# Attention on negated logits with one scaling a group, products issued in twos beside it, and the second tile's plain products in the sample's PSUM bank

## The chip, the cores and the metric

One core of one Trainium2 chip runs the whole step in one launch. The metric is the device time of that launch in microseconds. The kernel before took 1602.3 us, the median of three runs (1600.12, 1602.30, 1605.38).

## What is computed

One layer of a decoder trunk for 1024 prompt tokens and 8 x 4 sample tokens, d_model 1024, all in float32. The input projection has 9472 columns. Branch A is a gated linear recurrence (HGRN2, 8 heads). Branch B, which the change is about, is sliding-window attention with 16 query heads, 2 key-value heads of 64 channels, window 128, a learned sink for each head and a relative bias:

```python
def sink_softmax(logits, mask, sink):
    logits = jnp.where(mask, logits, -jnp.inf)
    m = jnp.maximum(jnp.max(logits, axis=-1, keepdims=True), sink)
    p = jnp.exp(logits - m)
    return p / (jnp.sum(p, axis=-1, keepdims=True) + jnp.exp(sink - m))
...
    logits = jnp.einsum('bnqkgd,bnskd->bnkgqs', qb, kk) * (B_HD ** -0.5)
    logits = logits + rel_bias_heads(rel, rel_bias)
    probs = sink_softmax(logits, mask, sink.astype(f32).reshape(B_KV_HEADS, B_GROUP, 1, 1))
    out = jnp.einsum('bnkgqs,bnskd->bnqkgd', probs, vv)
```

Both branches are gated and projected, merged, projected again, normalised and added to the residual. The projections behind the input projection (line 1391 on) are not touched.

## The kernel before

**Pairs.** The input projection goes by pairs of 128 output columns (`pair_gemm`, line 374). A pair is computed for two tiles of 512 tokens by Strassen-like products P1 to P7 over six of the eight blocks of the inner dimension; the two others go through `plain`. Every float32 operand is split into a high and a low part, so a product is three passes, and P1 to P7 are nine matmuls of 128 x 512 each, a `plain` six. All of them are recorded at line 380. In the rows, `HT`, `HB`, `LT`, `LB` with `wh`, `wl` are products of P1 to P7, `HR`, `LR` with `wrh`, `wrl` are `plain` ones.

**Banks.** Three PSUM banks `g0` to `g2` take the products, and a fourth, `gs`, has one buffer. `sample_products` (line 358) writes the 32 sample tokens' partial sums into it, ACT copies them out (line 365), and `sample_outputs` (line 368) writes the sums back into the same bank (line 370), from where the two epilogues of the pair read them. In the recurrence's pairs, `turned` (line 716) also allocates `gs`: it transposes the value projection, 32 sample rows first (line 730), then 128 x 512 tiles (line 734).

**Order within a pair** (lines 439 to 467): P1, the sample's products, P5, P6, `sample_outputs`, the second column block's plain products for the first tile (line 452, six matmuls), which DVE adds to the kept P5 (line 453), P3 with its plain, P7, P2 with its plain, P4 with its plain.

**Other work between the matmuls.** TensorE's order is the program's order. After every `quantum` matmuls of a pair, `tick()` (line 206) advances three queues of generators; a generator that yields n sleeps n ticks. Beside the heads of the recurrence (quantum 6) runs `hgrn_chain` (line 833); beside the eight attention pairs (line 1321) and the last four pairs (`gate_b`, line 1357) the quantum is `A_QUANTUM`, and attention is advanced: strip c has the query heads c and c + 8 and four groups of 256 queries. `rows_` (line 1206) issues `logits(g)` and sleeps `A_WAIT[0]` ticks; `outs` (line 1214) waits until the group's logits are issued, sleeps `A_WAIT[1]`, transposes the first half of the weights (`turn`, part 0), sleeps `A_WAIT[2]`, the second half, sleeps `A_WAIT[3]`, multiplies with the values, and sleeps `A_WAIT[4]`. An epilogue that must not run ahead of attention turns the queues itself (`settle`, line 1316). The other engines' orders are made by a scheduler from the recorded program.

**One group of attention.** TensorE writes two banks `lp` (lines 1151, 1155). DVE adds the relative bias and takes the row maximum against the sink, four times 128 x 256 (line 1159), negates the maxima (1161), adds the sink (1163, twice). ACT takes the exponentials with the negated maximum as bias and sums them (1167), and that of the sink (1164). DVE adds, inverts and scales (1169, 1170, 1172, four times). TensorE transposes through one bank `pt` (1182), ACT copies it out (1186), TensorE multiplies with the values (1197), DVE gates (1203). The query tile `stk` that the next strip's logits read is made by ACT (1334) and DVE (1335) out of the pair's first result (413).

## Time and profile before

| what | value |
|---|---|
| median of three runs | 1602.3 us |
| the profiled execution's own time | 1597.13 us |
| its span, first to last instruction | 1595.3 us |
| TensorE busy | 1519.1 us, 95% of the span |
| VectorE (DVE) busy | 956.5 us, 60% |
| ScalarE (ACT) busy | 667.2 us, 42% |
| GpSimd (POOL) busy | 415.9 us, 26% |
| mean granted TensorE clock | 0.978 of full speed |

The profile is of one execution. "Busy" of TensorE is modelled from pipelined matmuls. PEclk is the clock that was granted to TensorE, as a share of full speed. A group's row names line, engine and operation, then output and inputs by the program's names with shapes, then the count, then busy time and the mean of one in ns, then the engine's idle time just before them and what ended it. A row of the timeline has start and duration in us, and in brackets the idle time before it.

### The profile page before, as it was taken

What the parts mean: (1) busy time and instruction counts of PE and PEld (TensorE: products, weight loads), DVE (VectorE), ACT (ScalarE), POOL (GpSimd) and SP (SyncE); (2) the same over time, 40 slices, a digit from 0 to 9 for tenths busy, and PEclk for the clock granted to TensorE, in tenths of its full rate; (3) what the DMA queues carried; (4) which work ended last, traced back from release to release, by engine and by line L of the source; (5) the groups of instructions that cost most, each with busy time, mean ns of one, the idle gap of its engine ahead of it and who ended that gap; (6) DMA issues with size and microseconds to landing.
All of it is one profiled execution on the core that took longest, in us unless ns stands there. A gap on an engine that the chain in (4) does not pass through costs nothing. (4 is left out here: it accounts for less than half of the span.)

```text
span 1595.3 us, 27896 instructions
## 1 busy us (share of the span) xinstructions
PE 1519.1 (95%) x10569; PEld 1274.6 (80%) x10569; DVE 956.5 (60%) x2221; ACT 667.2 (42%) x1671; POOL 415.9 (26%) x381
## 2 busy tenths in 40 slices
PE   8999999999999999999789999999899999998998
PEld 8777777777787877777567677777699999997998
DVE  8777767575858585854567766764352244227532
ACT  6235343444444435354555555654331122333422
POOL 1374434444343435345111211213000000004100
PEclk9999999999999999999899999999989999998999
DMA  5212121213131212123111111133664544103321
GB/s 181 67 36 87 43 82 53 82 41 95 41 96 30 80 55 82 54 63 79 44 44 47 47 48 47 41 92 91 211 218 142 142 122 145 58 24 101 106 81 55
DMA packets 197250, 129.56 MB, mean 81 GB/s; under 512 B 46323, under 2 KB 184748, under 8 KB 197100
## 3 DMA queue, kind: packets, MB, share of 16 engines
q1 hardware_dynamic: 196300, 127.54, 26.8%
q8 instruction: 83, 1.36, 0.4%
q14 instruction: 51, 0.42, 0.1%
q0 software_dynamic: 672, 0.18, 0.1%
q10 hardware_dynamic: 144, 0.07, 0.0%
HBM read 96.89 MB, written 31.88 MB: 81 GB/s over the span
## 5 line engine op out<-in xcount | busy, mean ns | idle before, releaser
L268 POOL TENSOR_TENSOR wl<-raw,wh 128x384 fp32r<-128x384 f32 x106 | 113.6, 1074 | 272.1 <-ACT wh L267 246.8
L380 PE MATMUL g<-HT,wh 128*128 128x512 f32 x420 | 175.7, 418 | 0.0
L380 PE MATMUL g<-LT,wh 128*128 128x512 f32 x420 | 164.7, 392 | 0.0
L380 PE MATMUL g<-HT,wl 128*128 128x512 f32 x420 | 164.5, 392 | 0.0
L380 PE MATMUL g<-HB,wh 128*128 128x512 f32 x342 | 145.6, 426 | 9.5 <-DVE p L453 9.5
L380 PE MATMUL g<-HB,wl 128*128 128x512 f32 x342 | 136.4, 399 | 0.0
L380 PE MATMUL g<-LB,wh 128*128 128x512 f32 x342 | 136.2, 398 | 0.0
L268 DVE TENSOR_TENSOR wl<-ws,wh 128x384 fp32r<-128x384 f32 x136 | 94.8, 697 | 56.5 <-ACT wh L267 55.4
L267 ACT CAST wh<-ws 128x384 fp32r<-128x384 f32 x136 | 69.6, 512 | 128.1 <-PE g L380 88.1
L380 PE MATMUL g<-HR,wrh 128*128 128x512 f32 x288 | 120.8, 419 | 0.0
L380 PE MATMUL g<-HR,wrl 128*128 128x512 f32 x288 | 113.7, 395 | 0.0
L380 PE MATMUL g<-LR,wrh 128*128 128x512 f32 x288 | 113.1, 393 | 0.0
L380 PEld LDWEIGHTS g<-HT,wh 128*128 128x128 f32 x420 | 79.0, 188 | 33.4 <-issue 7.3
L267 ACT CAST wh<-raw 128x384 fp32r<-128x384 f32 x110 | 56.4, 514 | 106.4 <-PE g L380 97.9
L1571 POOL TENSOR_TENSOR yT<-yT,acc 128x1056 f32<-128x1056 f32 x4 | 12.9, 3262 | 319.4 <-ACT acc L1567 319.4
L380 PEld LDWEIGHTS g<-HT,wl 128*128 128x128 f32 x420 | 79.0, 188 | 17.7
L380 PEld LDWEIGHTS g<-HB,wh 128*128 128x128 f32 x342 | 65.8, 192 | 32.2 <-DVE p L453 12.5
L380 PEld LDWEIGHTS g<-LT,wh 128*128 128x128 f32 x420 | 79.3, 189 | 12.9
L1411 ACT CAST wh<-raw 128x1024 fp32r<-128x1024 f32 (+1 forms) x40 | 36.8, 920 | 124.0 <-PE g L1433 119.8
L380 PEld LDWEIGHTS g<-HB,wl 128*128 128x128 f32 x342 | 65.8, 192 | 15.1
L1412 DVE TENSOR_TENSOR wl<-raw,wh 128x1024 fp32r<-128x1024 f32 (+1 forms) x40 | 46.4, 1162 | 47.8 <-ACT wh L1411 47.8
L380 PEld LDWEIGHTS g<-LB,wh 128*128 128x128 f32 x342 | 66.0, 193 | 10.9
(392 smaller groups left out, 3986.4 us busy)
## 6 DMA issues: line engine op xcount, KB each, us to landing
raw<-in_w_in_dram SPq DMA_DIRECT2D x116, 256.0 KB
raw<-in_w_in_dram SPq DMA_DIRECT2D x64, 128.0 KB
oa_d<-G SPq DMA_DIRECT2D x8, 528.0 KB
oar<-oa_d SPq DMA_DIRECT2D x8, 528.0 KB
sga<-ga_d SPq DMA_DIRECT2D x8, 528.0 KB
obr<-ob_d SPq DMA_DIRECT2D x8, 528.0 KB
ma_d<-sga SPq DMA_DIRECT2D x8, 528.0 KB
gbr<-gb_d SPq DMA_DIRECT2D x8, 528.0 KB
```

What stands on the lines that cost most here:

```text
L267: S.copy(h, x)
L268: eng.tensor_tensor(l, x, h, op=ALU.subtract)
L380: T.matmul(ps, a, b, start=start, stop=stop, skip_group_check=True)
L1411: S.copy(wh[:, :kt, :], raw3)
L1412: V.tensor_tensor(wl[:, :kt, :], raw3, wh[:, :kt, :], op=ALU.subtract)
L1571: G.tensor_tensor(yT[i], yT[i], rb_, op=ALU.mult)
```

## The change

Five edits:

- Query tiles are scaled by -0.125 and the bias table by -1, so that DVE adds negated logits and keeps their minimum against a negated sink `nsink`. The minimum serves as the exponential's bias as it stands, with scale -1; the negation goes, and the two additions of the sink become one.
- The four scalings of a group become one `tensor_tensor` of 128 x 1024 with a broadcast operand (two for the first group of a strip).
- `turn` copies part 0 with DVE, part 1 with ACT as before.
- `A_QUANTUM` goes from 3 to 2 and `A_WAIT` from (5, 2, 2, 1, 2) to (7, 2, 2, 3, 1).
- The second column block's plain products for the first tile are written to bank `gs`; the third bank is no longer used at that place.

```diff
-A_QUANTUM = 3
-A_WAIT = (5, 2, 2, 1, 2)
+A_QUANTUM = 2
+A_WAIT = (7, 2, 2, 3, 1)
...
         if R:
-            b = bank(tb)
+            b = psg.tile([P, HT], F32, name=tname("g"), tag="gs", bufs=1)
             plain(b, 1, 0, True)
             V.tensor_tensor(p5, b, p5, op=ALU.add)
...
-        V.tensor_copy(rel, b[:16, :384])
+        V.tensor_scalar(rel, b[:16, :384], -1.0, None, op0=ALU.mult)
...
+    nsink = sp.tile([P, 16], F32, name="nsink", tag="ssh")
+    V.tensor_scalar(nsink, sink, -1.0, None, op0=ALU.mult)
...
-                    V.tensor_tensor_reduce(lg[:, j, w, lo:], bs[j][:, os], hank[:, j, ::-1][:, lo:], 1.0, sink[:, c + 8 * j:c + 8 * j + 1],
-                                           ALU.add, ALU.max, mx[:, 0, 2 * j + w:2 * j + w + 1])
-            V.tensor_scalar(mx[:, 1, :], mx[:, 0, :], -1.0, None, op0=ALU.mult)
-            for j in range(2):
-                V.tensor_scalar(mx[:, 2, 2 * j:2 * j + 2], mx[:, 1, 2 * j:2 * j + 2], sink[:, c + 8 * j:c + 8 * j + 1], None, op0=ALU.add)
+                    V.tensor_tensor_reduce(lg[:, j, w, lo:], bs[j][:, os], hank[:, j, ::-1][:, lo:], 1.0, nsink[:, c + 8 * j:c + 8 * j + 1],
+                                           ALU.add, ALU.min, mx[:, 0, 2 * j + w:2 * j + w + 1])
+            jw = lambda a: a.rearrange("p (j w) -> p j w", j=2)
+            V.tensor_tensor(jw(mx[:, 2, :]), jw(mx[:, 0, :]), jw(sink)[:, :, c:c + 1].broadcast_to([P, 2, 2]), op=ALU.add)
...
-                S.activation(lg[:, j, w, lo:], lg[:, j, w, lo:], AF.Exp, bias=mx[:, 1, 2 * j + w:2 * j + w + 1],
+                S.activation(lg[:, j, w, lo:], lg[:, j, w, lo:], AF.Exp, bias=mx[:, 0, 2 * j + w:2 * j + w + 1], scale=-1.0,
...
-            for j, w, lo in ji:
-                V.tensor_scalar(lg[:, j, w, lo:], lg[:, j, w, lo:], mx[:, 2, 2 * j + w:2 * j + w + 1], None, op0=ALU.mult)
+            mj = jw(mx[:, 2, :])
+            for ws, lo in ((slice(0, 2), 0),) if g else ((slice(0, 1), 128), (slice(1, 2), 0)):
+                l = lg[:, :, ws, lo:]
+                V.tensor_tensor(l, l, mj[:, :, ws, None].broadcast_to(list(l.shape)), op=ALU.mult)
...
-            S.copy(pT[:, :, lo:], b3[:, :, lo:])
+            (S.copy if part else V.tensor_copy)(pT[:, :, lo:], b3[:, :, lo:])
...
-                S.activation(s[r, j, :], ps[r], AF.Copy, scale=0.125)
-                V.scalar_tensor_tensor(s[o, j, :], ps[r], 0.125, s[r, j, :], op0=ALU.mult, op1=ALU.subtract)
+                S.activation(s[r, j, :], ps[r], AF.Copy, scale=-0.125)
+                V.scalar_tensor_tensor(s[o, j, :], ps[r], -0.125, s[r, j, :], op0=ALU.mult, op1=ALU.subtract)
```

From line 1104 on, lines of the changed kernel stand up to three further down (1182 becomes 1185).

Up to the last key-value pair, no engine's order of instructions changes but by the one negation of the sink; what changes there is who waits. Here is TensorE in the second pair of recurrence head 1, from the middle of the plain products at line 452 on; names in brackets are the engines whose progress a row waits for. Before:

```order
L380 MATMUL g185_1827<-LR7_282,wrh166_1711 128x512
L380 MATMUL g185_1827<-HR6_281,wrl167_1712 128x512
L866 MATMUL d186_1831<-QP1_1536,K1_1535 32x80 [waits DVE_49,PE_49]
L866 MATMUL d186_1831<-QP1_1536,K1_1535 32x80 x31
...
L380 MATMUL g176_1773<-HB228_294,wh171_1747 128x512 [waits Activation_49]
L380 MATMUL g176_1773<-LB229_295,wh171_1747 128x512
L380 MATMUL g176_1773<-HB228_294,wl172_1748 128x512
L730 MATMUL gt190_1892<-cst_118,ts183_1822 32x128 [waits PE_49,Activation_49]
```

And after:

```order
L380 MATMUL g185_1827<-LR7_282,wrh166_1711 128x512
L380 MATMUL g185_1827<-HR6_281,wrl167_1712 128x512 [waits DVE_49]
L866 MATMUL d186_1831<-QP1_1536,K1_1535 32x80 [waits DVE_49]
L866 MATMUL d186_1831<-QP1_1536,K1_1535 32x80 x31
...
L380 MATMUL g176_1773<-HB228_294,wh171_1747 128x512
L380 MATMUL g176_1773<-LB229_295,wh171_1747 128x512
L380 MATMUL g176_1773<-HB228_294,wl172_1748 128x512
L730 MATMUL gt190_1892<-cst_118,ts183_1822 32x128 [waits DVE_49]
```

The transposition of the sample's values (`gt`, line 730, bank `gs`) waited for readers of the sample's sums on ACT; now it waits for DVE, whose addition at line 453 is the last reader of the plain products (`g185`) that hold the bank.

In the third pair of the same head, where the plain products follow the sample's sums. Before, and then after:

```order
L748 MATMUL d224_2174<-cst_118,K1_1535 32x128 [waits Activation_49]
...
L370 MATMUL gs212_2107<-cst_118,part213_2116 128x32 x2
L380 MATMUL g228_2193<-HR6_281,wrh205_2001 128x512
L380 MATMUL g228_2193<-LR7_282,wrh205_2001 128x512
L380 MATMUL g228_2193<-HR6_281,wrl206_2002 128x512
```

```order
L748 MATMUL d224_2174<-cst_118,K1_1535 32x128 [waits Activation_49]
...
L370 MATMUL gs212_2107<-cst_118,part213_2116 128x32 x2
L380 MATMUL g228_2193<-HR6_281,wrh205_2001 128x512 [waits Activation_49]
L380 MATMUL g228_2193<-LR7_282,wrh205_2001 128x512
L380 MATMUL g228_2193<-HR6_281,wrl206_2002 128x512
```

The order is the same, and the first plain product has got a wait for ACT, which reads the sample's sums out of the bank.

TensorE in attention, ahead of the transposition (`pt5_1_0`) of strip 5's second group, whose logits are `lp5_1`. Before, with the rows between left out (the logits of group 3, `lp5_3`, are already issued):

```order
L1155 MATMUL lp5_3_1_10331<-KL_7711,stk5_1_10090 128x256
L380 MATMUL g1259_10206<-HR6_281,wrh1250_10101 128x512
L380 MATMUL g1259_10206<-LR7_282,wrh1250_10101 128x512
...
L1197 MATMUL po5_0_10361<-pTs_7970,vN_7712 64x128 x2
L380 MATMUL g1252_10170<-HT34_268,wh1260_10207 128x512
...
L1182 MATMUL pt5_1_0_10394<-cst_118,lg5_1_10119 128x128 x4
L1182 MATMUL pt5_1_1_10400<-cst_118,lg5_1_10119 128x128 x4
```

After:

```order
L1157 MATMUL lp5_1_1_10043<-KL_7711,stk5_0_9950 128x256
L380 MATMUL g1241_10002<-HR6_281,wrl1217_9711 128x512
L380 MATMUL g1241_10002<-HR6_281,wrh1216_9710 128x512
L380 MATMUL g1241_10002<-LR7_282,wrh1216_9710 128x512
L380 MATMUL g1241_10002<-HR6_281,wrl1217_9711 128x512
L380 MATMUL g1218_9777<-HT490_1234,wh1235_9913 128x512
L380 MATMUL g1218_9777<-LT491_1235,wh1235_9913 128x512
L380 MATMUL g1218_9777<-HT490_1234,wl1236_9914 128x512
L380 MATMUL g1218_9777<-HT490_1234,wh1235_9913 128x512
L380 MATMUL g1218_9777<-LT491_1235,wh1235_9913 128x512
L380 MATMUL g1218_9777<-HT490_1234,wl1236_9914 128x512
L1185 MATMUL pt5_1_0_10097<-cst_118,lg5_1_10040 128x128 x4
```

Before, 66 matmuls of line 380 and the logits of two further groups stand between `lp5_1` and `pt5_1_0`; after, ten matmuls and nothing else. From strip 1 on, the four groups of a strip have 6, 10, 11 and 16 matmuls of line 380 between their logits and their first transposition; the third has in addition a product with the values and the sample's products, the fourth a product with the values and the sample's sums. The first group's logits come four matmuls behind the last plain product of P3.

## The prediction

> **What bounds the kernel now.** The page's first rows, then the windows of two stages, recurrence and attention strips.

> ```profile
> span 1595.3 us, 27896 instructions
> ...
> PE 1519.1 (95%) x10569; PEld 1274.6 (80%) x10569; DVE 956.5 (60%) x2221; ACT 667.2 (42%) x1671; POOL 415.9 (26%) x381
> ...
> 130.00:745.00 615.00, 596.57 (x4761) 471.56 (x4761) 421.59 (x864) 269.04 (x713) 259.00 (x245) 1.00 0.22 65
> 754.00:1050.00 296.00, 271.80 (x1585) 202.25 (x1586) 206.68 (x681) 166.32 (x489) 53.02 (x53) 0.95 0.18 45
> ```

> In a window's row, after its bounds and length stand the busy times of TensorE's matmuls, its weight loads, DVE, ACT and POOL, then the granted clock. TensorE is busy for 97% of the recurrence and 92% of attention, so a wait of TensorE is added time and work elsewhere is hidden while it keeps ahead. The execution took 1597.13 us, 1.8 more than its span and 5.2 less than the median of the runs. What TensorE waits for, in attention (first three rows) and in the whole run (the last):

> ```profile
> PE pt L1182 <- ACT pTs L1186: 11.3, 6, 2.2
> PE pt L1182 <- DVE lg L1172: 7.2, 2, 4.5
> PE lp L1151 <- DVE stk L1335: 4.3, 9, 0.9
> ...
> PE g L380 <- DVE p L453: 9.5, 7, 1.4
> ```

> Total, times and longest follow the colon. Attention also loses clock, 5% of 296 us, 14.8. So all that this change could win by shorter waits is 11.3 + 7.2 + 4.3 + 9.5 + 14.8 = 47 us.

> **The bank.** The plain products of line 452 now wait until both epilogues have read the sample's sums, and whoever takes the bank next waits for line 453. The second pair of a head:

> ```profile
> 409.36:419.92 10.56, 9.24 (x103) 7.13 (x101) 10.54 (x21) 2.56 (x7) 5.97 (x6) 1.00 0.18 51
> ...
> 409.81 0.48 PE L380 MATMUL g<-HR,wrh 128*128 128x512 f32 x1
> ...
> 410.09 0.20 ACT L811 ACTIVATE G<-gs 128x32 f32<-128x32 f32 x1
> ...
> 413.54 0.27 PE L730 MATMUL gt<-cst,ts 128*32 128x128 f32 x1
> ...
> 418.21 0.39 PE L380 MATMUL g<-HT,wl 128*128 128x512 f32 x1
> ...
> 419.15 0.77 DVE L453 TENSOR_TENSOR p<-g,p 128x512 f32<-128x512 f32 x1
> ...
> 419.97 0.51 PE L380 MATMUL g<-HB,wh 128*128 128x512 f32 x1 [1.38 <-DVE p L453]
> ```

> DVE is busy for 10.54 of the 10.56 us up to the end of line 453: it works off the recurrence's chain, which stands ahead in its order, unchanged. Today only P2 waits for that addition, 1.38 us. After, the transposition at 413.54 waits until 419.92, and behind it on TensorE stand P3's last six matmuls, its plain and P7, which run until 418.60 today, 5.06 us. P2 no longer waits, so it starts 5.0 us later; DVE then waits for P3 and stays as far behind TensorE as now. The wait of 0.5 us for the sample's readers (to 410.29) falls inside. Seven heads: 35.0 us.

> The other two pairs of a head wait for the sample's readers alone (third pair, first pair, and the first pair of head 1, where DVE still makes the differences of the input tiles):

> ```profile
> 440.56 0.48 PE L380 MATMUL g<-HR,wrh 128*128 128x512 f32 x1
> ...
> 441.73 0.21 ACT L821 ACTIVATE ct<-gs 128x32 f32<-128x32 f32 x1
> ...
> 470.47 0.48 PE L380 MATMUL g<-HR,wrh 128*128 128x512 f32 x1
> ...
> 471.86 0.17 DVE L773 TENSOR_TENSOR QP<-gs,ct 128x8 f32<-128x8 f32 x1
> ...
> 137.69 0.48 PE L380 MATMUL g<-HR,wrh 128*128 128x512 f32 x1
> ...
> 142.18 0.16 DVE L773 TENSOR_TENSOR QP<-gs,ct 128x8 f32<-128x8 f32 x1
> ```

> 441.94 less 440.56 is 1.4, seven times; 472.03 less 470.47 is 1.6, six times; 142.34 less 137.69 is 4.65 once. That is 9.8 + 9.6 + 4.65 = 24 us. The key-value pair and the last pairs, by the 0.5 us above, make 2. Sum of the bank's waits: 61 us.

> **The clock after a wait.** A wait of 1.99 us, and TensorE's rows some microseconds later:

> ```profile
> 949.73 0.66 PE L1182 MATMUL pt<-cst,lg 128*128 128x128 f32 x4 [1.99 <-ACT pTs L1186]
> ...
> 951.70:955.11 3.41, 3.41 (x18) 2.39 (x17) 2.52 (x13) 0.89 (x3) 0.74 (x1) 0.50 0.04 12
> ...
> 954.23 0.63 PE L380 MATMUL g<-LB,wh 128*128 128x512 f32 x1
> ...
> 954.66 0.60 PE L380 MATMUL g<-HB,wl 128*128 128x512 f32 x1
> ...
> 955.34 0.40 PE L380 MATMUL g<-LB,wh 128*128 128x512 f32 x1
> ...
> 955.57 0.40 PE L380 MATMUL g<-HB,wl 128*128 128x512 f32 x1
> ```

> For 3.41 us the clock is granted at half, and matmuls follow each other by 0.43 us in place of 0.23: 3.41 x (1 - 0.23 / 0.43) = 1.6 us lost. The waits of 1.38 us brought none (the recurrence's window has a clock of 1.00). I charge 1.6 for each new wait of about 2 us or more: seven second pairs and the one of 4.65, so 8 x 1.6 = 13. The bank costs 74 us. [...]

> **Twos and the new waits.** Today a group's softmax has 66 matmuls of cover. Only the first strip shows what it takes uncovered, the first group with 9 matmuls between, the second with 15:

> ```profile
> 762.63 0.47 PE L1182 MATMUL pt<-cst,lg 128*128 128x128 f32 x1 [4.53 <-DVE lg L1172]
> ...
> 769.31 0.50 PE L1155 MATMUL lp<-KL,stk 64*128 64x256 f32 x4
> ...
> 770.04 0.48 DVE L1159 CUSTOM_DVE_ANT_0 lg<-lp,hank,sink 128x256 f32<-128x256 f32 x1
> ...
> 771.26 0.48 DVE L1159 CUSTOM_DVE_ANT_0 lg<-lp,hank,sink 128x256 f32<-128x256 f32 x1
> ...
> 772.71 0.51 ACT L1167 ACTIVATE lg<-lg,mx 128x256 f32<-128x256 f32 x1 [0.24 <-DVE mx L1161]
> ...
> 775.10 0.18 DVE L1170 RECIPROCAL mx<-mx 128x4 f32<-128x4 f32 x1
> ...
> 775.65 1.14 DVE L1172 TENSOR_SCALAR lg<-lg,mx 128x256 f32<-128x256 f32 x4
> ...
> 776.15 1.03 PE L1182 MATMUL pt<-cst,lg 128*128 128x128 f32 x4 [2.69 <-DVE lg L1172]
> ```

> From the logits' end at 769.81 to the last scaling at 776.79 are 7.0 us, and TensorE waited 4.53 and 2.69. After the change every group is like these, with less cover. What the edits take from the chain: without the negation the exponentials start behind the first reduction in place of the fourth. With free engines: reductions to 1.75 us after the logits, exponentials to 2.5, the sink's to 2.7, sum and reciprocal to 3.1, scaling to 4.3. The scaling itself wins nothing; the rows for it and for what else stands in the queues:

> ```profile
> L1412 DVE TENSOR_TENSOR wl<-raw,wh 128x1024 fp32r<-128x1024 f32 x32 | 39.7, 1244 | 44.3 <-ACT wh L1411 44.3
> ...
> L268 DVE TENSOR_TENSOR wl<-ws,wh 128x384 fp32r<-128x384 f32 x136 | 94.8, 697 | 56.5 <-ACT wh L267 55.4
> ...
> L413 DVE TENSOR_TENSOR ct<-g,u 128x512 f32<-128x512 f32 x34 | 23.6, 693 | 31.6 <-PE g L380 31.5
> ...
> L1335 DVE SCALAR_TENSOR_TENSOR stk<-ct,stk 64x512 fp32r<-64x512 f32 x32 | 21.9, 686 | 3.9 <-ACT stk L1334 3.2
> ...
> L1334 ACT ACTIVATE stk<-ct 64x512 fp32r<-64x512 f32 x32 | 20.1, 629 | 16.9 <-DVE ct L413 16.5
> ```

> One scaling of 1.2 us stands for four that took 1.14 together, and TensorE could start behind the first of those. The engines are not free: their orders put other work inside the chain. For a strip:

> - First group: reductions to 1.5, exponentials and a weight cast on ACT to 2.9, the sink's to 3.1; then DVE has a weight split, the sum, a gate (0.69) and the reciprocal to 4.7, the scaling to 5.8. Cover 6 x 0.23 = 1.4; wait 4.4.
> - Second: reductions to 1.8, line 413 to 2.5, on ACT half of the query tile to 3.2 and the sink's to 3.4; on DVE half of the query tile to 4.0, the sum, the other half to 4.8, the reciprocal, the scaling to 6.2. Cover 10 x 0.23 = 2.3; wait 3.9.
> - Third: two weight splits stand ahead of the last three reductions, which end at 2.6; a gate to 3.3, a cast and the sink's on ACT to 4.2, another split to 4.6, sum and reciprocal to 4.9, scaling to 6.1. Cover 11 x 0.23, a product with the values (some 0.8) and the sample's (1.0), 4.2; wait 1.9.
> - Fourth: 4.3, but DVE has the sample's last reader behind the scaling, and the bank keeps TensorE for that: 4.9 against 4.0; wait 0.9.
> - Query tile: the strip's first logits stand four matmuls (0.9) behind the result that they need, by way of lines 413, 1334 twice and 1335: 0.69 + 1.26 + 0.69 and some latency, 3.0; wait 2.1.

> Sum 13.2 a strip. Three of these bring half clock that is not itself covered: 4.8. Eight strips: 8 x 18.0 = 144. What goes is today's 11.3 + 7.2 + 4.3 + 14.8 = 38. Net +106. POOL and the loads are a product further ahead of TensorE and gain time from every wait; the bias tables are issued a strip ahead as now. DVE's part-0 copy, at line 453's 0.7 us, fits the four matmuls before part 1.

> **Sum.** 1597.1 + 74 + 106 = 1777; the medians lie up to 5 us above, so I say 1780. Bounds: the chain at 4.3 everywhere gives waits of 2.9 + 2.0 + 0.1 + 0.9 + 2.1 = 8.0 with two half clocks, 8 x 11.2 - 38 = +52; at today's 7.0, 5.6 + 4.7 + 2.8 + 3.0 + 2.1 = 18.2 with four, 8 x 24.6 - 38 = +159. The bank is 61 without any half clock and 84 if the six waits of 1.6 have it too. So 1597 + 61 + 52 = 1710 to 1597 + 84 + 159 = 1840. Of the rivals I take in the one at 1703, and say 1700 to 1835.

> **Rivals.**

> - Faster: the shorter chain and the even spacing end today's waits, and none take their place: 1597 - 47 = 1550. Decides if the chain falls below its cover of 1.4 to 4.2 us and line 453 comes before the transposition. Against it, four reductions alone take 1.7, and DVE has 10.5 us of work ahead of line 453. Chance 0.02.
> - Attention comes out even, its waits as long as today's: 1597 + 74 = 1671. It needs a chain of about 3 us; no row is that short. 0.06.
> - The bank costs nothing, since the scheduler's work ahead of line 453 is not what holds it: 1597 + 106 = 1703. Against it, DVE's unbroken 10.54 us. 0.05.
> - The half clock stays on through attention: some 34 us of matmuls a strip at half rate lose 34 x 0.47 = 16 in place of 4.8, 8 x 11 = 90 more, 1870. In the rows it ends within 3.4 us once TensorE is dense. 0.07.
> - [...] 0.10. [...]
> - Both parts stay covered and nothing changes: 1602, for the reasons of the first rival less likely still. 0.01.

> My forecast has the other 0.69; outside the range lie 0.02 + 0.06 + 0.07 + 0.01 = 0.16. A measurement tells about 0.3%, 5 us, from no change: faster 0.02, same 0.01, slower 0.97.

> **What would show it.** Right: line 730 waiting for line 453 some 6 us, seven times; `HR` products waiting for lines 821 and 773; `pt` part 0 waiting 4 us for the scaling in the first two groups of every strip; the attention window some 400 us in place of 296, its clock about 0.9. Wrong: the last pairs or the projections behind them longer, the first transpositions of a group without waits, or line 453 early on DVE.

## The result and the profile after

The changed kernel takes 1782.1 us (median of four runs, 1780.5 to 1783.2) against 1602.4 for the kernel before: a ratio of 1.112, 95% interval 1.110 to 1.114. The profiled execution took 1781.36 us. The page's head, and its row of the granted clock in 40 slices:

```profile
span 1779.6 us, 27734 instructions
...
PE 1578.7 (89%) x10569; PEld 1307.9 (73%) x10569; DVE 956.5 (54%) x2102; ACT 656.2 (37%) x1639; POOL 425.8 (24%) x381
...
PEclk9999999999999999998888888889997999999999
```

The attention slices, 19 to 27, stand at 8 where the others stand at 9, but for one, slice 31 right behind the last pairs, where the kernel before dips too. The windows of four stages follow: the recurrence from head 1's first sums of the sample on with the key-value pair, the eight strips, the last pairs, the rest. Columns as in the prediction: bounds, length, busy times of TensorE's matmuls and weight loads, DVE, ACT and POOL, then the clock.

```profile
143.64:823.94 680.30, 612.05 (x4742) 482.48 (x4740) 411.07 (x857) 264.33 (x698) 254.08 (x242) 0.96 0.19 58
823.94:1231.63 407.69, 320.89 (x1685) 229.45 (x1684) 219.90 (x591) 164.25 (x488) 62.92 (x58) 0.86 0.14 36
1231.63:1314.96 83.33, 76.52 (x463) 59.61 (x461) 33.55 (x81) 30.50 (x70) 20.30 (x20) 0.98 0.43 135
1314.96:1779.60 464.64, 443.22 (x2711) 430.31 (x2709) 190.19 (x304) 131.99 (x222) 23.92 (x9) 0.97 0.36 109
```

The same stages of the kernel before:

```profile
137.33:746.44 609.11, 592.41 (x4741) 468.63 (x4740) 415.57 (x856) 264.21 (x698) 255.33 (x244) 1.00 0.22 65
746.44:1051.40 304.96, 279.98 (x1624) 208.71 (x1623) 210.31 (x685) 169.84 (x497) 58.43 (x58) 0.95 0.19 47
1051.40:1132.64 81.24, 81.24 (x524) 63.20 (x523) 37.88 (x107) 37.07 (x94) 19.40 (x20) 1.00 0.37 117
1132.64:1595.30 462.66, 443.00 (x2711) 430.57 (x2709) 189.46 (x304) 131.32 (x222) 23.95 (x9) 0.97 0.38 114
```

So +71.2 in the recurrence, +102.7 in attention, +2.1 in the last pairs, +2.0 in the rest, and +6.3 ahead of 143.64: 184.3 together. What TensorE waits for now (total, times, longest):

```profile
PE pt L1185 <- DVE lg L1175: 65.7, 31, 3.9
PE gt L730 <- DVE p L453: 36.0, 7, 5.2
PE lp L1153 <- DVE stk L1338: 13.8, 16, 1.3
PE g L380 <- DVE QP L773: 12.6, 7, 3.0
PE g L380 <- ACT ct L821: 8.9, 7, 1.3
...
PE ckp L1261 <- DMA cK<-in_cache_swa_k_dram: 5.4, 1, 5.4
...
PE g L380 <- POOL wl L268: 4.9, 1, 4.9
...
PE g L380 <- DVE zS L1354: 4.8, 8, 0.6
PE g L380 <- ACT G L811: 2.8, 7, 0.5
```

The first transposition of the first three groups of every strip waits for the scaling, the transposition of the sample's values waits for line 453, and the readers of the sample's sums hold the plain products up. The wait of P2 for line 453 is gone. Of the rows that the prediction did not have, the 4.9 us for POOL stand at 64.7 in the start-up; of the other traces only no_bank's shows them, and most kernels without them have the same code there, so they are not laid to the change. The second pair of head 4 in the changed kernel, TensorE and DVE:

```profile
449.99 0.50 PE L380 MATMUL g<-HR,wrh 128*128 128x512 f32 x1 [0.37 <-ACT G L811]
...
453.50 0.40 PE L380 MATMUL g<-HB,wl 128*128 128x512 f32 x1
...
458.22 0.77 DVE L453 TENSOR_TENSOR p<-g,p 128x512 f32<-128x512 f32 x1
459.04 0.39 PE L730 MATMUL gt<-cst,ts 128*32 128x128 f32 x1 [5.14 <-DVE p L453]
```

TensorE stands still from 453.90 to 459.04, until the addition of line 453 has let the bank go. The second group of a settled strip (from the second on, the strips repeat alike), TensorE, DVE and ACT:

```profile
1052.00 0.50 PE L1157 MATMUL lp<-KL,stk 64*128 64x256 f32 x4
...
1052.54 0.48 DVE L1161 CUSTOM_DVE_ANT_0 lg<-lp,hank,nsink 128x256 f32<-128x256 f32 x1 [0.66 <-PE lp L1157]
...
1054.61 0.39 PE L380 MATMUL g<-HT,wl 128*128 128x512 f32 x1
...
1055.79 0.63 ACT L1337 ACTIVATE stk<-ct 64x512 fp32r<-64x512 f32 x1
...
1056.61 0.69 DVE L1338 SCALAR_TENSOR_TENSOR stk<-ct,stk 64x512 fp32r<-64x512 f32 x1
1057.33 0.18 DVE L1171 RECIPROCAL mx<-mx 128x4 f32<-128x4 f32 x1
1057.54 1.23 DVE L1175 TENSOR_TENSOR lg<-lg,mx 128x1024 f32<-128x1024 f32 x1
...
1058.91 0.63 PE L1185 MATMUL pt<-cst,lg 128*128 128x128 f32 x4 [3.91 <-DVE lg L1175]
```

From the end of the logits at 1052.50 to the end of the scaling at 1058.77 are 6.3 us, with the query tile's halves (lines 1337 and 1338) inside, and ten matmuls do not cover them: the last of them ends at 1055.00, and TensorE stands for 3.91.

### The profile page after: what moved, and what is told of

Same layout as the page of the kernel before. It is cut to its first block, busy times and chain, and to the rows that moved or that the text cites. A ratio compares the mean times of both kernels' runs of the same rounds, so it can differ in the third digit from the quotient of the medians.

```text
span 1779.6 us, 27734 instructions
## 1 busy us (share of the span) xinstructions
PE 1578.7 (89%) x10569; PEld 1307.9 (73%) x10569; DVE 956.5 (54%) x2102; ACT 656.2 (37%) x1639; POOL 425.8 (24%) x381
## 5 line engine op out<-in xcount | busy, mean ns | idle before, releaser
L268 POOL TENSOR_TENSOR wl<-raw,wh 128x384 fp32r<-128x384 f32 x106 | 125.7, 1189 | 329.4 <-ACT wh L267 319.4
L380 PE MATMUL g<-HT,wh 128*128 128x512 f32 x420 | 174.1, 414 | 0.0
L380 PE MATMUL g<-HT,wl 128*128 128x512 f32 x420 | 169.8, 404 | 0.0
L380 PE MATMUL g<-LT,wh 128*128 128x512 f32 x420 | 169.7, 404 | 0.0
L380 PE MATMUL g<-HR,wrh 128*128 128x512 f32 x288 | 124.4, 432 | 31.6 <-DVE QP L773 12.6
L380 PE MATMUL g<-HB,wh 128*128 128x512 f32 x342 | 151.1, 442 | 0.0
L380 PE MATMUL g<-HB,wl 128*128 128x512 f32 x342 | 146.0, 427 | 4.9 <-POOL wl L268 4.9
L380 PE MATMUL g<-LB,wh 128*128 128x512 f32 x342 | 146.7, 429 | 0.0
L268 DVE TENSOR_TENSOR wl<-ws,wh 128x384 fp32r<-128x384 f32 x136 | 94.7, 697 | 91.3 <-ACT wh L267 90.0
L267 ACT CAST wh<-ws 128x384 fp32r<-128x384 f32 x136 | 69.6, 512 | 146.4 <-PE g L380 129.6
L380 PE MATMUL g<-LR,wrh 128*128 128x512 f32 x288 | 119.9, 416 | 0.0
L380 PE MATMUL g<-HR,wrl 128*128 128x512 f32 x288 | 117.9, 409 | 0.0
L1185 PE MATMUL pt<-cst,lg 128*128 128x128 f32 x240 | 50.0, 332 | 68.3 <-DVE lg L1175 65.7
L267 ACT CAST wh<-raw 128x384 fp32r<-128x384 f32 x110 | 56.2, 513 | 142.3 <-PE g L380 135.6
L380 PEld LDWEIGHTS g<-HT,wh 128*128 128x128 f32 x420 | 79.7, 190 | 29.4 <-issue 7.0
L1185 PEld LDWEIGHTS pt<-cst,lg 128*128 128x128 f32 x240 | 32.7, 166 | 91.9 <-issue 80.0
L380 PEld LDWEIGHTS g<-HT,wl 128*128 128x128 f32 x420 | 80.9, 193 | 19.1 <-issue 1.4
L380 PEld LDWEIGHTS g<-HR,wrh 128*128 128x128 f32 x288 | 58.1, 202 | 46.7 <-ACT ct L821 9.7
L380 PEld LDWEIGHTS g<-LT,wh 128*128 128x128 f32 x420 | 80.4, 191 | 15.6
L380 PEld LDWEIGHTS g<-HB,wl 128*128 128x128 f32 x342 | 70.8, 207 | 19.9 <-POOL wl L268 5.4
```

Source lines behind the costliest of these rows:

```text
L267: S.copy(h, x)
L268: eng.tensor_tensor(l, x, h, op=ALU.subtract)
L380: T.matmul(ps, a, b, start=start, stop=stop, skip_group_check=True)
L1185: T.transpose(b3[:, j, P * w:P * w + P], lgs[g][:, j, w, half:half + P], ident)
```

## The experiments

Each kernel ran beside the kernel before on the same chip; the ratios are to those runs, with their 95% intervals. The kernel before had medians of 1600.2 to 1600.7 us there.

| kernel | median us | ratio | interval |
|---|---|---|---|
| bank_alone | 1696.6 | 1.061 | 1.059 to 1.063 |
| no_bank | 1703.1 | 1.066 | 1.063 to 1.068 |
| softmax_alone | 1591.1 | 0.995 | 0.993 to 0.997 |
| twos_alone | 1727.6 | 1.080 | 1.077 to 1.082 |
| bank_act | 1645.4 | 1.027 | 1.024 to 1.031 |
| lag | 1602.0 | 1.001 | 0.9995 to 1.003 |
| lag_d4b | 1585.5 | 0.990 | 0.987 to 0.993 |
| extra | 1691.9 | 1.057 | 1.053 to 1.061 |
| softmax_act | 1575.8 | 0.985 | 0.983 to 0.987 |
| lag_d4b_act | 1573.8 | 0.984 | 0.982 to 0.985 |
| no_bank_four | 1688.3 | 1.055 | 1.053 to 1.057 |
| extra_plain | 1702.0 | 1.064 | 1.062 to 1.066 |

**bank_alone.** The kernel before with this edit alone:

```diff
-            b = bank(tb)
+            b = psg.tile([P, HT], F32, name=tname("g"), tag="gs", bufs=1)
```

> The kernel before, with only the plain products of line 452 moved to the sample's bank. Theory (two independent costs): the recurrence's waits come as in the changed kernel, 36 us for line 453 ahead of line 730, 24 us for the sample's readers, and their half clock, and attention stays near 305 us: 1602 + 74 to 80 = 1676 to 1682. Rival (the recurrence lost its time to something else, or only together with the attention edits): 1602. Second rival (the sample's readers in the shared bank also upset attention, which waits for line 1354 in the changed kernel): attention longer by 10 us or more, 1690 and up.

Measured 1696.6, 96 us slower, which is the second rival. Its windows of recurrence and attention, and its waits:

```profile
137.48:821.11 683.63, 612.69 (x4741) 482.59 (x4740) 413.63 (x856) 264.21 (x698) 254.96 (x244) 0.97 0.19 58
821.11:1148.55 327.44, 288.77 (x1623) 214.87 (x1622) 209.72 (x685) 169.83 (x497) 58.37 (x58) 0.92 0.17 44
```

```profile
PE gt L730 <- DVE p L453: 35.9, 7, 5.2
PE g L380 <- DVE zS L1351: 18.6, 8, 4.5
```

The recurrence is 74.5 us longer than before, as in the changed kernel. Attention is 22 longer too: with the old order TensorE waits up to 4.5 us there for the sample's last reader, line 1351 on DVE, and half clock follows (0.92 in place of 0.95). The prediction did not have this; in the changed kernel that wait is 0.6 a strip.

**no_bank.** The changed kernel with that one line back at `bank(tb)`.

> The changed kernel with the plain products of line 452 back in the third bank. Theory: the recurrence takes 590 us again, attention stays 100 us longer than before: 1782 - 76 = 1706. If attention's strips are held to whole multiples of the 3.41 us in which the clock is granted (they take 51.2 us each, 15 times 3.413), the 0.6 us of the wait for line 1354 either change nothing (1706) or take a whole step of 3.41 off each strip (1706 - 27 = 1679). Rival (the bank is what holds attention up too): attention near 305 us, 1602.

Measured 1703.1, 102 us more than before. It has 9.6 us of P2's old wait and the rows of the changed kernel in attention:

```profile
PE pt L1185 <- DVE lg L1175: 68.8, 31, 3.9
...
PE g L380 <- DVE p L453: 9.6, 7, 1.4
```

Attention takes 405.3 us with strips of 51.2, though the wait for line 1354 is gone: first of the two ways that the theory left open. Bank and order are two costs. Each has its own stage, 74 us in the recurrence and 102 in attention, and so far they add. But the bank's 22 us in attention come with the old order only: the bank costs 96 there (bank_alone) and 79 with the new one (1782.1 less 1703.1).

**softmax_alone.** The edits of the softmax with products in threes, the old waits and the old bank:

```diff
-A_QUANTUM = 2
-A_WAIT = (7, 2, 2, 3, 1)
+A_QUANTUM = 3
+A_WAIT = (5, 2, 2, 1, 2)
...
-            b = psg.tile([P, HT], F32, name=tname("g"), tag="gs", bufs=1)
+            b = bank(tb)
```

> The kernel before with the negated logits, the one scaling and DVE's copy of part 0, but products in threes, the old waits and the old bank. Theory (the lost time of attention comes from the order, not from these edits): the chain is about a us shorter and seldom uncovered, so 1592 to 1605, no change to slightly faster. Rival (the one scaling or DVE's copy, queued behind DVE's other work, makes the waits): 10 us or more slower, 1612 to 1700.

1591.1, 0.3 to 0.7% faster. The softmax edits do not carry the loss. What attention waits for most here is another row:

```profile
PE pt L1185 <- DVE pTs L1189: 13.4, 7, 3.0
```

**twos_alone.** The kernel before with the two constants:

```diff
-A_QUANTUM = 3
-A_WAIT = (5, 2, 2, 1, 2)
+A_QUANTUM = 2
+A_WAIT = (7, 2, 2, 3, 1)
```

> The kernel before with only the two constants changed (products in twos, the new waits). Theory: the order alone takes the cover away, and with the old, about 1 us longer chain the waits are longer than in the changed kernel: 1602 + 106 + 8 x 1 to 8 x 3.4 = 1716 to 1735, strips of 51.2 or 54.6 us. Rival (the loss needs the new softmax): 1602 to 1650.

1727.6, 127 us slower, strips of 54.6 us; the rival falls. The order alone takes the cover away, and with the old softmax it is 24.5 us worse than with the new (no_bank). The first transpositions wait for the old scalings as they do for the new one:

```profile
PE pt L1182 <- DVE lg L1172: 81.9, 40, 5.0
```

**bank_act.** bank_alone, but the plain products leave the bank by ACT:

```diff
-            V.tensor_tensor(p5, b, p5, op=ALU.add)
+            t = ctile()
+            S.copy(t, b)
+            V.tensor_tensor(p5, t, p5, op=ALU.add)
```

> The kernel before with the plain products in the sample's bank, as in bank_alone, but ACT copies them to SBUF at once, and DVE adds the copy. Theory (line 730 waits because line 453 stands behind 10 us of DVE's other work; ACT's copy stands right behind that of u2): the 36 us for line 730 go, and their half clock with them (41 us of half clock, some 19 us lost), the 24 us for the sample's readers stay: 1697 - 36 - 19 = 1642. Rival (the bank is taken twice in a pair and any reader is too late, or the copy holds ACT up and TensorE waits for something else instead): 1680 to 1700.

1645.4, 51 us less than bank_alone where 55 were expected. Two lines further down line 730 is 732; its row for line 453 is gone, and the readers of the sample's sums are still waited for:

```profile
PE g L380 <- DVE zS L1353: 18.9, 8, 4.4
PE g L380 <- DVE QP L775: 12.2, 7, 3.1
...
PE gt L732 <- ACT G L813: 0.7, 1, 0.7
```

That shows the cause of the recurrence's largest wait: DVE's other work ahead of line 453 held the bank, not the bank's double use as such. Of the 45 us that are left, 20 lie in the recurrence (628.6 us), where the readers of the sums are waited for, and 22 in attention, which is as long as in bank_alone (327.2 us).

**lag.** The changed kernel with the old bank and one condition more in `outs`:

```diff
-                yield until(("logits", n))
+                yield until(("logits", min(n + 1, 31)))
```

> The changed kernel with the old bank, and each group's first transposition held back until the logits of the next group are issued, so that 28 to 44 matmuls stand between a group's logits and its transposition in place of 6 to 16. Theory (only the cover was missing): the waits for line 1175 (69 us) go, those of the logits for the query tile (14 us) stay; without any wait a strip is 305 less 38, 267 us for eight, so attention takes 281 to 294 and the run 1577 to 1590, faster than both kernels. Rival (products in twos themselves, or DVE's longer queue, hold attention up): 1600 or more.

1602.0, no different from before: a miss by 12 to 25 us. The waits for the scaling are gone from the list, which cover was meant to do, but others take their place:

```profile
PE lp L1153 <- DVE stk L1338: 13.6, 16, 1.3
PE pt L1185 <- DVE pTs L1189: 10.8, 8, 1.6
```

The 10.8 us for DVE's copy of part 0 I had not reckoned with, nor four stretches of half clock behind the query tile's wait (3.41 x 4 x 0.47 = 6.4; the window's clock is 0.98). Then some 276 us of dense work remain of its 308.8 in attention, where I had put 267. Some 4 of these 9 us can be the 42 small matmuls more that its window holds (1666 for 1624, at an estimated 0.1 us each: in the changed kernel four transpositions take 0.39 us, from 1058.91 to the next matmul at 1059.30); the rest is left open.

**lag_d4b.** As lag, with

```diff
-A_WAIT = (7, 2, 2, 3, 1)
+A_WAIT = (7, 2, 3, 3, 1)
...
-                enqueue(parts_[0](range(2)), 1, q=1)
+                enqueue(parts_[0](range(2)), 4, q=1)
...
-                enqueue(parts_[0](range(2, 4)), 1, q=1)
+                enqueue(parts_[0](range(2, 4)), 4, q=1)
```

> As lag, and the logits of a query tile are issued four steps after it in place of one, the second half of a group's transpositions six matmuls after the first in place of four. Theory: the 14 us for the query tile go as well, attention comes near 270 us and the run to 1562 to 1580. Rival (as for lag): 1600 or more; a third way, the same time as lag within 5 us, if its waits for the query tile were already hidden by other waits.

1585.5, 1% faster than before, 5 us above what was expected. The query tile's 13.6 us have left the list's head; DVE's copy stays:

```profile
PE pt L1185 <- DVE pTs L1189: 9.3, 6, 2.9
```

**extra.** no_bank with work added:

```diff
+        if quantum == A_QUANTUM:
+            prepared_w, prepared_x = W.v["P2"][0], X.v["B21"][0]
+            for _ in range(4):
+                T.matmul(b, prepared_w[:, 0, :], prepared_x[:, 0, :], start=True, stop=False, skip_group_check=True)
         product(b, "P2", "B21", True)
```

> no_bank with the first matmul of P2 issued four times more in each pair of attention and of the gates behind it: 0.9 us of dense work in a strip, its result overwritten. Theory (a strip settles on a whole multiple of the 3.41 us grid of the clock): every settled strip is again 51.20 us, or 54.61: the run 1703 + 2 to 4, or 1703 + 27 + 3. Rival (work simply adds): strips of 52.1 us, the run 1703 + 10 = 1713.

1691.9: more work made it 11 us faster, which neither theory had. The four matmuls stand between a strip's first logits and their transposition and are cover for the first group. The row of the waits for the scaling fell to 57.9 us (it stands four lines lower than in no_bank, where it was 68.8):

```profile
PE pt L1189 <- DVE lg L1179: 57.9, 31, 3.9
```

As a test of the clock's grid it was misplaced; it speaks for the missing cover as the cause of attention's loss. extra_plain repeats it elsewhere.

**softmax_act.** softmax_alone with ACT's copy:

```diff
-            (S.copy if part else V.tensor_copy)(pT[:, :, lo:], b3[:, :, lo:])
+            S.copy(pT[:, :, lo:], b3[:, :, lo:])
```

> softmax_alone with ACT's copy of part 0 again, so that the kernel before is changed only by the negated logits and the one scaling. Theory (the copy's engine makes no difference, ACT's waits of 11 us before against DVE's of 13 us in softmax_alone): 1587 to 1595, as softmax_alone. Rival (DVE's copy costs, because it stands behind DVE's other work): 1575 to 1584; second rival (DVE's copy is what made softmax_alone faster): 1600.

1575.8: the theory falls, the first rival holds. DVE's copy costs 15 us, and negated logits with one scaling, without it, win 1.5% over the kernel before.

```profile
PE pt L1185 <- ACT pTs L1189: 4.6, 6, 1.5
```

**lag_d4b_act.** The same line changed in lag_d4b.

> lag_d4b with ACT's copy of part 0 in place of DVE's. lag_d4b waits 9.3 us for DVE's copies and has 10 us of half clock in attention. Theory (DVE works off four reductions and splits of weights, ACT a queue of exponentials just as long): the waits change engine and stay, 1580 to 1590. Rival (ACT has the room): these waits and their half clock go, 1570 to 1577.

1573.8, the rival again. The copy's waits fall from 9.3 to 5.9, and attention has no half clock left (clock 1.00, 279 us where the kernel before takes 305):

```profile
PE pt L1185 <- ACT pTs L1189: 5.9, 7, 1.8
```

```profile
746.73:1025.86 279.13, 270.50 (x1646) 199.52 (x1645) 198.56 (x546) 174.35 (x507) 64.07 (x58) 1.00 0.20 52
```

This is the fastest kernel of the study, at 0.883 of the changed kernel's time (1573.8 / 1782.1); softmax_act's interval overlaps its own.

**no_bank_four.** no_bank with the old scalings:

```diff
-            mj = jw(mx[:, 2, :])
-            for ws, lo in ((slice(0, 2), 0),) if g else ((slice(0, 1), 128), (slice(1, 2), 0)):
-                l = lg[:, :, ws, lo:]
-                V.tensor_tensor(l, l, mj[:, :, ws, None].broadcast_to(list(l.shape)), op=ALU.mult)
+            for j, w, lo in ji:
+                V.tensor_scalar(lg[:, j, w, lo:], lg[:, j, w, lo:], mx[:, 2, 2 * j + w:2 * j + w + 1], None, op0=ALU.mult)
```

> no_bank with the four scalings of a group in place of the one. Theory (the one scaling of 1.23 us wins nothing against four pieces, and the first transposition need not wait for the last piece): 1703 or a little less, 1690 to 1705. Rival (the one scaling is what makes the softmax edits 24 us faster than twos_alone): 1715 to 1728.

1688.3, 15 us less than no_bank, 2 under the foot of the theory's range. Where a transposition waits, four pieces let it start behind the first (the row's total is 54.9 us in place of 68.8, its longest 3.6 in place of 3.9), and the one scaling is a loss:

```profile
PE pt L1183 <- DVE lg L1173: 54.9, 32, 3.6
```

**extra_plain.** The four matmuls ahead of the plain products, where nothing waits for a softmax:

```diff
+            if quantum == A_QUANTUM:
+                for _ in range(4):
+                    T.matmul(b, W.v["R"][0][:, 0, 0, 1, :], X.v["R"][0][:, 0, :HT], start=True, stop=False, skip_group_check=True)
             plain(b, 1, 0, True)
```

> As extra, but the four added matmuls stand ahead of the plain products of line 452, behind P5 and P6 of each pair of attention and of the gates, not between a group's logits and its transposition that waits: 0.9 us of dense work in a strip that covers no wait. Theory (the clock's half rate follows the fixed 3.41 us grid, and a strip near a multiple of it settles there): strips of 51.20 or 54.61 us, 1703 to 1706 or about 1733. Rival (work adds, the grid only shifts which window is halved): strips of 52.1 us on the mean, changing from strip to strip, about 1713.

1702.0, the same as no_bank, a little under the theory's range. The sample's sums of three strips in a row:

```profile
1001.21 0.53 PE L370 MATMUL gs<-cst,part 128*128 128x32 f32 x4
...
1052.41 0.53 PE L370 MATMUL gs<-cst,part 128*128 128x32 f32 x4
...
1103.62 0.53 PE L370 MATMUL gs<-cst,part 128*128 128x32 f32 x4
```

51.20 and 51.21: the added 0.9 us a strip are not seen, because a settled strip now has three stretches of half clock, 10.2 us, where no_bank's has 13.7.

## Why the prediction was right

The time, 1782 for 1780, and the two mechanisms were right: bank_alone, bank_act, twos_alone and lag show each alone. That the time came within 2 us is luck, since several terms were off and made up for each other. The two stages lost 71 and 103 us where 74 and 106 were forecast; the start-up and the last stages lost 10 that the sum did not have; and the 3 us added for the medians were 0.8 (1782.1 against the profiled 1781.4). The range's top was put at 1835 where its own sum gives 1840.

- Second pairs: line 730 was to wait some 6 us and P2's wait to go, 5.0 net, with the wait for the sample's readers inside. Line 730 waited 5.14, and the readers (line 811) took 0.4 ahead of it: 36.0 + 2.8 - 9.5 is 29.3 for seven pairs in place of 35.0. The step that was off: I held DVE's chain fixed against TensorE. From the first plain product to the start of line 453 were 419.15 - 409.81 = 9.3 us before; now they are 458.22 - 449.99 = 8.2. Of these 1.1 us, 0.4 are the readers' wait, which starts TensorE later, and 0.5 are DVE's line 875, which took 0.69 us here and 1.19 before.
- Waits for the sample's readers in the other pairs: 12.6 + 8.9 = 21.5 in the place of 24. Head 1's first pair waited 3.0 of the 4.65.
- Half clock in the recurrence: 13 was charged, one stretch of 3.41 us for each of eight long waits. From 143.64 on, nine stretches make 47.8 us, of which 12.5 lie in waits; 35.3 x 0.47 is 17. Five of the seven second pairs brought two stretches' length, head 1's wait of 3.0 us none, and two waits of 1.55 and 1.84 us for line 773, which the sum had put at nothing, one each. Waits and clock, 29.3 + 21.5 + 17 = 68, against +71 in the window.
- Attention, one settled strip: first group 3.4 + 0.2 (4.4 predicted), second 3.9 (3.9), third 1.2 (1.9), the sample's last reader 0.6 (0.9), query tile 1.3 + 0.4 (2.1), 11.0 together for 13.2. The chains came out as drawn (6.3 for 6.2 in the second); what was mis-sized most is the first group's cover, which I counted at full clock and most of which runs in a half-clock stretch. Half clock is 13.7 us a strip, 3.6 of it in a wait: 10.1 x 0.47 = 4.7 for the 4.8 predicted. All waits of the window are 87 us, with 8 x 4.7 for the clock 125; less the old 38, +87 where +103 were measured. Some 6 of the other 16 are 61 small matmuls more in the window (1685 for 1624, at the same estimated 0.1 us each), which earlier fell into the last pairs.
- What a wait costs beside its length: matmuls follow each other by 0.23 us, but one that a wait follows counts for its whole 0.39 (the one at 1054.61, behind which the wait is counted from 1055.00), so a wait takes an estimated 0.16 more than its row says. Attention has 56 waits where the kernel before had 18, 38 x 0.16 = 6; the recurrence has 38 for 16, 22 x 0.16 = 3.5, which closes its 68 to 71. Some 4 us of attention are not placed.
- "The scaling itself wins nothing": no_bank_four shows that it loses 15 us in this order. "DVE's part-0 copy fits": in the changed kernel it does, and no row of the waits names it; in the orders with cover it costs 12 to 15 us (softmax_act, lag_d4b_act).
- The rivals: faster, even attention, a free bank and no change are out by the windows. The half clock did not stay on through attention, but left after one to three stretches of 3.41 us. No run shows what the chance of 0.10 was given to: half clock followed a wait of 1.55 us too, in rows below.
- Not foreseen: 5.4 us for the sample's cache (line 1261), whose load is reached earlier now that no group lags behind; the row stands in all six traces with the new order and its short cover, and in no other. The last pairs are 2.1 us longer with it.

## What to carry to other kernels

Before an order is made more even, count for each dependent step the work that stands between it and what it waits for: the backlog that looks untidy may be the cover, and here two constants that removed it cost 127 us (twos_alone), while one condition won 101 back (lag against no_bank). The bank that was given a second use was held until its last reader's turn in that engine's queue came (5.14 us in a head for line 453 on DVE; with ACT as the reader, bank_act, the run took 51 us less than bank_alone), so look at the queue, and let the engine with the shortest one empty it. Merging operations is worth nothing while the waiting engine could start on the first piece: here it lost 15 us (no_bank against no_bank_four). And what an edit is worth depends on the order around it: the softmax edits won 10 us with the old order (softmax_alone) and 24.5 with the new (no_bank against twos_alone), and the bank cost 96 and 79.

## What the runs showed of the hardware

```profile
238.95 0.47 PE L380 MATMUL g<-HR,wrh 128*128 128x512 f32 x1 [1.54 <-DVE QP L773]
...
332.07 0.47 PE L380 MATMUL g<-HR,wrh 128*128 128x512 f32 x1 [1.55 <-DVE QP L773]
```

```profile
329.80:333.21 3.41, 1.86 (x11) 1.56 (x10) 0.64 (x4) 2.40 (x9) 2.53 (x3) 1.00 0.01 3
333.21:336.62 3.41, 3.41 (x14) 2.79 (x12) 0.69 (x1) 0.00 (x0) 0.48 (x1) 0.50 0.49 145
237.64:241.05 3.41, 2.10 (x9) 1.75 (x10) 1.07 (x5) 1.45 (x5) 1.86 (x2) 1.00 0.01 2
241.05:244.46 3.41, 3.41 (x20) 2.77 (x19) 1.58 (x3) 0.52 (x1) 0.16 (x1) 1.00 0.54 160
```

The wait at 332.07 lies wholly in one stretch, leaves it 1.55 us idle, and the next stretch is at half; the one at 238.95 is parted 0.23 to 1.31, and nothing follows. 241.05 to 333.21 is 27 times 3.413, and all half-clock stretches of this trace begin on that grid. Of the grid's stretches at full clock between 130 and 1320 us, all 16 with over 1.9 us idle were followed by half clock, of those with 1.2 to 1.84 some (11) and some (16) not; what decides there is open. Head 1's wait of 3.04 us, parted 1.31 to 1.73 by an edge of the grid, was not followed by any. A stretch about half idle was enough here (1.55 of 3.41 us).

In six runs strips that repeat with half clock in each come out at whole multiples of these 3.413 us. The changed kernel, no_bank and extra_plain settle at 51.20 us a strip, 15 times 3.413; twos_alone at 54.6, 16 times; two strips of no_bank_four, from 943.07 to 1042.04, make 98.97, 29 times; three of extra, from 842.97 to 989.69, make 146.72, 43 times. So small savings or costs in such a stage may vanish, as the added work of extra_plain did, or come out as a step of 3.4 us a strip, as between no_bank and twos_alone.
